# Rings of four buffers for split weights, and a later place in the code for the second memory split

## The chip, the cores and the metric

The kernel runs on one core of one Trainium2 chip. The metric is the device time of one execution in microseconds (us), the median of three runs. The engines are TensorE (PE, its weight loads PEld), VectorE (DVE), ScalarE (ACT), GpSimd (POOL) and SyncE (SP, which issues the weight loads from HBM here).

## The reference

A decoder trunk of two layers works on 512 tokens of width 1024, in float32. Each layer has a mixer, a cross-attention over 256 memory tokens and a SwiGLU feed-forward network (FFN) with 2816 hidden units, each behind an RMSNorm and with a residual add.

```python
def swiglu(h, w_gate_up, w_down):
    g, u = jnp.split(h @ w_gate_up, 2, axis=-1)
    return (jax.nn.silu(g) * u) @ w_down

for layer in range(DEPTH):                      # DEPTH = 2
    if layer % 2 == 0:                          # pooling mixer beside latent attention (MLA)
        x = x + even_mixer(rms_norm(x, ev_norm[j]), ...)
    else:                                       # Griffin: conv, gates, RG-LRU scan, GeLU gate
        x = x + odd_mixer(rms_norm(x, od_norm[j]), reset, ...)
    x = x + mem_cross_attention(rms_norm(x, xa_norm_x[layer]), mem, xa_norm_mem[layer], ...)
    x = x + swiglu(rms_norm(x, ffn_norm[layer]), ffn_w_gate_up[layer], ffn_w_down[layer])
return rms_norm(x, final_norm)
```

## The kernel before

Activations are kept transposed, features on the partitions: eight tiles of 128 x 512 for `x`. Each float32 operand is split into a high part `hi`, rounded to the type that TensorE takes in one pass, and the remainder `lo`. A product is then three matmuls per 128 rows of depth (`mm3`): L169 `hi` with `hi`, L170 `hi` of the weight with `lo` of the activation, L171 `lo` of the weight. ScalarE makes each `hi` by a copy (L101 for a weight, L156 for other tiles, L159 with a gain), VectorE makes each `lo` (L102, L157, L160).

`Weights.get` loads a block of weights into one of two raw buffers (`wraw`), on SP, and splits it into one buffer of the ring `whi` and one of the ring `wlo`. Both rings belong to the whole kernel: every projection of it and the fast FFN tiles draw from them. A buffer is free again when the last matmul that reads it has run.

The FFN has 22 hidden tiles per layer, in five parts of 4, 4, 4, 4 and 6. While a part's hidden tiles are made, the down projection of the part before it runs, two of its eight output tiles (names `s`) per hidden tile; its weights are the `dn` blocks (`dn_h`, `dn_l`), one block per two outputs. The last part has its down projection alone at the end of the FFN, one block per output. Tiles 5 to 21 of layer 0 and 5 to 15 of layer 1 are made by `fast`: two products of the full size are replaced by seven of a quarter of it, with 12 matmuls of 128 x 256 each. In the order of the code these are f1 (bank X, with names `mm`), f2 (Y, `tr`), f4 (Z, `att`), f5 (X), f7 (Z), f6 (X) and f3 (X). Their weights come in four splits (`parts`, names `sw_h` and `sw_l`): f1|f2 from a loaded half `gr`, f4|f6 from a sum `sa`, f5|f7 from a sum `sb`, and f3 from the other loaded half. With the `dn` block a fast tile takes five buffers of each ring. What I call a period is the work of one fast tile with its two down outputs.

The tile at the end of `fast` is multiplied with the SiLU of the gate and split (`hidden`; `act` in the trace), for the down projection.

Behind layer 0's last fast tile, `fastp.close()` gives up the pool of the fast tiles. `aside` is the function `ready` of the main program: it opens the pool `mg1`, loads the memory tokens into `keys` (four loads on SP) and splits them with the gain of layer 1's memory norm into `mg` (eight L159 on ScalarE, eight L160 on VectorE, of 128 x 256). `mg` is first read in the odd layer, by `mem_keys` (names `mg`, `xk_h`), whose products wait for banks that VectorE empties with `g` (L1044). L1057 multiplies gates and scanned states there, L1036 is the scan, and L278 the residual add anywhere.

No order of instructions is written out here. The scheduler of the tile framework takes the code's order as a list, estimates times, and gives each engine a fixed sequence; dependencies and free buffers decide which instruction is next in it.

Of the kernel before, what the change touches and what calls it, by code (L numbers as in the profile page):

```python
# [71 lines left out]
class Weights:  # L72


    def __init__(self, kern, ap, name, parts=None, low=None, into=None):
        self.kern, self.ap, self.name, self.into = kern, ap, name, into
        self.low = low or kern.nc.vector
        self.pools = parts or (kern.wraw, kern.whi, kern.wlo)
        self.n, _, self.F = ap.shape
        self.group = max(1, 1024 // self.F)  # L80
        self.raw = {}
        self.parts = {}
# [24 lines left out]
class Trunk:  # L107
    def __init__(self, ctx, tc, ins, out):
        self.ctx, self.tc, self.nc, self.ins, self.out = ctx, tc, tc.nc, ins, out
        pool = lambda name, bufs=1, **kw: ctx.enter_context(tc.tile_pool(name=name, bufs=bufs, **kw))  # L110
        self.cst = pool("cst")
        self.xp = pool("xp")
        self.kfp = pool("kfp")
        self.wraw = pool("wraw", 2)
        self.whi = pool("whi", 3)
        self.wlo = pool("wlo", 3)
        self.inp = pool("inp", 4)
        self.actp = pool("act", 16)
        self.tp = pool("tmp", 2)
        self.rp = pool("rp", 1)  # L120
        self.sm = pool("sm", 12)
        self.psum = pool("psum", 2, space=PSUM)
        self.uid = 0
        self.flip = 0
# [637 lines left out]
    def ffn(self, layer, nrm, nxt_spec, aside=None):  # L762
# [107 lines left out]
        def down(p, hs):  # L870
            nf = FFN_PARTS[p]
            W = Weights(self, ins[f"ffn_down{p}"], f"dn{layer}_{p}")
            n = D // (nf * P)
            return [lambda m=m: self.linear(W, layer * (KD // n) + m // n, hs, off=m % n * nf * P, bank="s")
                    for m in range(KD)]
# [4 lines left out]
        for p, nf in enumerate(FFN_PARTS):  # L880
            last = p == len(FFN_PARTS) - 1
            if last and final:
                fastp.close()
                pool = self.ctx.enter_context(self.tc.tile_pool(name="tail", bufs=1))
# [26 lines left out]
            for f in range(f0 + len(hs), f0 + nf):  # L911
                hs.append(fast(f, st) if f in FAST[not final] else plain(f))
                for _ in range(2):
                    if todo:
                        m = KD - len(todo)
# [5 lines left out]
            self.tail(Wd, hs, layer * KD, B)  # L921
            return None
        fastp.close()
        if aside:
            aside()
        nxt = self.next_norm(B, *nxt_spec)
        for m, run in enumerate(down(p, hs)):
            self.residual(m, run(), nxt)
        return nxt

    def odd(self, nrm, nxt_spec):
# [302 lines left out]
```

## Time and profile before

| | |
|---|---|
| median of three runs | 1410.14 us (1410.04 to 1410.41) |
| profiled execution | 1408.14 us |
| its span, first to last instruction | 1406.3 us |
| mean granted TensorE clock | 0.992 of full speed |
| TensorE busy | 1368.2 us, 97% of the span |
| VectorE busy | 910.8 us, 65% |
| ScalarE busy | 652.7 us, 46% |
| bytes moved by DMA | 139.40 MB, 99 GB/s on average |

Busy time of TensorE counts matmuls whose spans overlap, so 97% is not 97% of what it could do: the distance from one start to the next tells its pace. In the rows below, a time stands first for the start and then for the length; what is in brackets at the end is how long the engine was idle just before, and what ended that.

### The profile page before, as it was taken

The numbers are of one execution on the slowest core, as the hardware profiler recorded it, in microseconds if no ns is written. First come the engines' busy times: TensorE is split into PE (matmuls) and PEld (weight loads), VectorE is DVE, ScalarE is ACT, GpSimd is POOL, SyncE is SP. The second block draws the span as 40 slices with busy tenths as digits, with TensorE's granted clock in tenths as the row PEclk, the third lists the DMA queues.
The fourth block names the chain that finished last, engine by engine and source line by source line (L and its number), as shares of the span: only waits on it lengthen the run. The fifth ranks groups of instructions, "written<-read, shape, count | busy, mean of one in ns | idle before, by whom it ended". The sixth has DMA issues, their size and how long they took to land.

```text
span 1406.3 us, 19022 instructions
## 1 busy us (share of the span) xinstructions
PE 1368.2 (97%) x7496; PEld 1176.1 (84%) x7496; DVE 910.8 (65%) x1449; ACT 652.7 (46%) x1053; POOL 119.3 (8%) x131
## 2 busy tenths in 40 slices
PE   8899999999999999999999989999999999999998
PEld 7678788878888999989788878888888889998887
DVE  6787574545777767676868696445559676764343
ACT  6477653444444344444544754335445334443231
POOL 0431021003000000000110001211120000000001
PEclk9989999999999999999999999999999999999999
DMA  6231162323242332331232234322324233213231
GB/s 208 81 94 57 57 187 82 106 75 105 86 139 90 107 104 90 103 93 53 90 105 91 89 99 157 98 71 89 117 90 143 83 105 106 91 46 113 97 106 60
DMA packets 44970, 139.40 MB, mean 99 GB/s; under 512 B 5584, under 2 KB 9808, under 8 KB 44880
## 3 DMA queue, kind: packets, MB, share of 16 engines
q1 hardware_dynamic: 43440, 136.86, 30.2%
q10 hardware_dynamic: 1440, 1.32, 0.3%
q8 instruction: 59, 0.97, 0.3%
q14 instruction: 31, 0.25, 0.1%
HBM read 135.93 MB, written 2.10 MB: 98 GB/s over the span
## 4 chain that ended last, share of the span: by engine, by line
PE 81%; ACT 7%; DVE 5%; issue 3%; DMA 2%; POOL 0%; POOLq 0%; DVEq 0%; ACTq 0%
PE mm L169 14%; PE mm L170 13%; PE mm L171 13%; PE s L171 6%; PE att L169 6%; PE att L170 6%; PE att L171 5%; PE s L169 5%; PE s L170 5%; ACT sw_h L156 2%; ACT dn_h L101 1%; ACT t L855 1%; PE tr L170 1%; PE tr L169 1%; PE tr L171 1%
## 5 line engine op out<-in xcount | busy, mean ns | idle before, releaser
L169 PE MATMUL s<-act,dn_h 128*128 128x512 f32 x304 | 118.7, 391 | 2.1 <-ACT act L156 1.6
L170 PE MATMUL s<-act,dn_h 128*128 128x512 f32 x304 | 118.7, 390 | 0.6 <-DVE act L157 0.6
L171 PE MATMUL s<-act,dn_l 128*128 128x512 f32 x304 | 116.7, 398 | 0.0
L250 POOL TENSOR_TENSOR ssq<-ssq,t 128x512 f32<-128x512 f32 (+1 forms) x37 | 57.7, 1560 | 632.3 <-ACT t L249 632.0
L156 ACT CAST sw_h<-sa 128x1024 fp32r<-128x1024 f32 x28 | 29.4, 1049 | 138.3 <-PE s L170 131.5
L278 DVE TENSOR_TENSOR x<-s,x 128x512 f32<-128x512 f32 x72 | 49.5, 688 | 51.5 <-PE s L171 51.4
L101 ACT CAST gu_h<-gu_raw 128x1024 fp32r<-128x1024 f32 x32 | 33.6, 1051 | 85.6 <-PE mm L170 45.4
L171 PEld LDWEIGHTS s<-act,dn_l 128*128 128x128 f32 x304 | 57.0, 188 | 14.0 <-DVE dn_l L102 1.9
L169 PEld LDWEIGHTS s<-act,dn_h 128*128 128x128 f32 x304 | 57.2, 188 | 12.9 <-ACT act L156 2.1
L170 PEld LDWEIGHTS s<-act,dn_h 128*128 128x128 f32 x304 | 57.1, 188 | 12.1 <-DVE act L157 1.0
L101 ACT CAST dn_h<-dn_raw 128x1024 fp32r<-128x1024 f32 (+1 forms) x40 | 40.2, 1007 | 51.8 <-PE att L170 30.7
L171 PE MATMUL mm<-tb,sw_l 128*128 128x256 f32 x224 | 63.5, 284 | 0.0
L170 PE MATMUL mm<-tb,sw_h 128*128 128x256 f32 x224 | 63.4, 283 | 0.0
L169 PE MATMUL mm<-tb,sw_h 128*128 128x256 f32 x224 | 62.8, 281 | 0.0
L854 DVE TENSOR_TENSOR t<-att,pc 128x256 f32<-128x256 f32 x28 | 11.9, 424 | 77.2 <-PE att L171 77.2
L102 DVE TENSOR_TENSOR gu_l<-gu_raw,gu_h 128x1024 fp32r<-128x1024 f32 x32 | 39.2, 1224 | 25.4 <-ACT gu_h L101 24.9
L157 DVE TENSOR_TENSOR sw_l<-gr,sw_h 128x1024 fp32r<-128x1024 f32 (+1 forms) x56 | 53.2, 950 | 1.1 <-ACT sw_h L156 0.8
L156 ACT CAST sw_h<-gr 128x1024 fp32r<-128x1024 f32 (+1 forms) x56 | 46.4, 828 | 15.4 <-PE mm L170 6.1
L169 PE MATMUL mm<-act,gu_h 128*128 128x512 f32 x128 | 50.3, 395 | 0.0
L169 PE MATMUL mm<-act,xq_h 128*128 128x512 f32 x128 | 50.1, 391 | 0.0
L171 PE MATMUL mm<-act,xq_l 128*128 128x512 f32 x128 | 50.1, 391 | 0.0
L169 PE MATMUL att<-act,gu_h 128*128 128x512 f32 x128 | 50.0, 390 | 0.0
(478 smaller groups left out, 4462.1 us busy)
## 6 DMA issues: line engine op xcount, KB each, us to landing
gr<-in_ffn_gu_dram SPq DMA_DIRECT2D x56, 512.0 KB, 3.6
gu_raw<-in_ffn_gu_dram SPq DMA_DIRECT2D x32, 512.0 KB, 3.5
dn_raw<-in_ffn_down_dram SPq DMA_DIRECT2D x32, 512.0 KB, 3.5
xk_raw<-in_xa_w_k_dram SPq DMA_DIRECT2D x16, 512.0 KB, 3.5
xq_raw<-in_xa_w_q_dram SPq DMA_DIRECT2D x16, 512.0 KB, 3.5
xv_raw<-in_xa_w_v_dram SPq DMA_DIRECT2D x16, 512.0 KB, 3.5
xo_raw<-in_xa_w_o_dram SPq DMA_DIRECT2D x16, 512.0 KB, 3.6
odin_raw<-in_od_w_in_dram SPq DMA_DIRECT2D x16, 512.0 KB, 3.5
```

Of the source, the lines that this page charges most:

```text
L101: nc.scalar.copy(hi, src)
L102: self.low.tensor_sub(lo, src, hi[:, :].bitcast(F32))
L156: nc.scalar.copy(hi, src)
L157: nc.vector.tensor_sub(lo, src, hi.bitcast(F32))
L169: nc.tensor.matmul(out, wh, xh, start=begin and i == 0, stop=False, **kw)
L170: nc.tensor.matmul(out, wh, xl, start=False, stop=False, **kw)
L171: self.mm_ins = nc.tensor.matmul(out, wl, xh, start=False, stop=end and i == last, **kw).ins
L250: (low or nc.gpsimd).tensor_add(ssq[:, :n], ssq[:, :n], sq[:, :n])
L278: self.nc.vector.tensor_add(self.x[m], ps, self.x[m] if src is None else src)
L854: nc.vector.tensor_add(t[:, hi], Z, c[:, hi])
L855: nc.scalar.activation(t, t, AF.Silu)
```

## The change

Both rings of split weights get a fourth buffer. The call of `aside` moves from ahead of the last down projection of layer 0 to behind its second output tile.

```diff
@@ -112,8 +112,8 @@
         self.xp = pool("xp")
         self.kfp = pool("kfp")
         self.wraw = pool("wraw", 2)
-        self.whi = pool("whi", 3)
-        self.wlo = pool("wlo", 3)
+        self.whi = pool("whi", 4)
+        self.wlo = pool("wlo", 4)
         self.inp = pool("inp", 4)
         self.actp = pool("act", 16)
         self.tp = pool("tmp", 2)
@@ -921,11 +921,11 @@
             self.tail(Wd, hs, layer * KD, B)
             return None
         fastp.close()
-        if aside:
-            aside()
         nxt = self.next_norm(B, *nxt_spec)
         for m, run in enumerate(down(p, hs)):
             self.residual(m, run(), nxt)
+            if m == 1 and aside:
+                aside()
         return nxt
 
     def odd(self, nrm, nxt_spec):
```

The scheduler makes a new order from this. Three places of it matter below. In the rows, numbers tell buffers apart; what stands right of the arrow is read.

In the fast stage of layer 0 this stands on ScalarE, for one period; `pc` (L846, L850, L852) are copies of banks, `t0` (L855) is the SiLU, and 753, 755 and 776 are banks. Before:

```order
L846 COPY pc_756_4222<-mm_753_4219 128x256
L156 CAST act0_737_4155<-t1_736_4061 128x512
L156 CAST sw_h_751_4215<-gr_742_4195 128x512
L850 COPY pc_757_4223<-att_755_4221 128x256
L852 COPY pc_756_4222<-mm_753_4219 128x256
L101 CAST dn0_0_h2_4325<-dn0_0_raw2_4323 128x1024
L855 ACTIVATE t0_758_4224<-t0_758_4224 128x512
L156 CAST sw_h_766_4361<-gr_764_4357 128x1024
L156 CAST sw_h_769_4368<-sa_768_4365 128x1024
L156 CAST sw_h_772_4375<-sb_771_4372 128x1024
L846 COPY pc_779_4386<-mm_776_4383 128x256
```

After:

```order
L156 CAST sw_h_751_4215<-gr_742_4195 128x512
L156 CAST act0_737_4155<-t1_736_4061 128x512
L846 COPY pc_756_4222<-mm_753_4219 128x256
L101 CAST dn0_0_h2_4325<-dn0_0_raw2_4323 128x1024
L850 COPY pc_757_4223<-att_755_4221 128x256
L852 COPY pc_756_4222<-mm_753_4219 128x256
L156 CAST sw_h_766_4361<-gr_764_4357 128x1024
L855 ACTIVATE t0_758_4224<-t0_758_4224 128x512
L156 CAST sw_h_769_4368<-sa_768_4365 128x1024
L156 CAST sw_h_772_4375<-sb_771_4372 128x1024
L156 CAST sw_h_774_4379<-gr_765_4359 128x512
```

The down block's split `dn0_0_h2` moves ahead of the copies L850 and L852, and f1's split `sw_h_766` ahead of the SiLU. TensorE's order at the same place, from the end of f6 (`sw_h_746`) to the next tile's f1 (`sw_h_766`), before:

```order
L169 MATMUL mm_753_4219<-ta_694_3777,sw_h_746_4204 128x256
L170 MATMUL mm_753_4219<-ta_695_3778,sw_h_746_4204 128x256
L171 MATMUL mm_753_4219<-ta_694_3777,sw_l_747_4205 128x256
L169 MATMUL s_762_4329<-act0_668_3715,dn0_0_h2_4325 128x512
L170 MATMUL s_762_4329<-act0_669_3716,dn0_0_h2_4325 128x512
L169 MATMUL s_763_4343<-act0_668_3715,dn0_0_h2_4325 128x512
L170 MATMUL s_763_4343<-act0_669_3716,dn0_0_h2_4325 128x512
L169 MATMUL mm_776_4383<-act1_652_3676,sw_h_766_4361 128x256
L170 MATMUL mm_776_4383<-act1_653_3677,sw_h_766_4361 128x256
L169 MATMUL tr_777_4384<-act1_660_3696,sw_h_766_4361 128x256
```

After, from the end of f7 (`sw_h_749`) to the start of f6 (`sw_h_746`):

```order
L169 MATMUL att_755_4221<-act1_666_3711,sw_h_749_4211 128x256
L170 MATMUL att_755_4221<-act1_667_3712,sw_h_749_4211 128x256
L171 MATMUL att_755_4221<-act1_666_3711,sw_l_750_4212 128x256
L171 MATMUL s_762_4329<-act0_668_3715,dn0_0_l2_4326 128x512
L169 MATMUL s_762_4329<-act0_672_3725,dn0_0_h2_4325 128x512
L170 MATMUL s_762_4329<-act0_673_3726,dn0_0_h2_4325 128x512
L171 MATMUL s_762_4329<-act0_672_3725,dn0_0_l2_4326 128x512
L169 MATMUL s_762_4329<-act0_702_3851,dn0_0_h2_4325 128x512
L169 MATMUL mm_753_4219<-ta_676_3735,sw_h_746_4204 128x256
L170 MATMUL mm_753_4219<-ta_677_3736,sw_h_746_4204 128x256
```

The other ten matmuls of f6 and 13 of the down projection follow; then come its last two and the next tile's f1:

```order
L170 MATMUL s_763_4343<-act0_709_3922,dn0_0_h2_4325 128x512
L171 MATMUL s_763_4343<-act0_708_3921,dn0_0_l2_4326 128x512
L169 MATMUL mm_776_4383<-act1_652_3676,sw_h_766_4361 128x256
L170 MATMUL mm_776_4383<-act1_653_3677,sw_h_766_4361 128x256
L169 MATMUL tr_777_4384<-act1_660_3696,sw_h_766_4361 128x256
L170 MATMUL tr_777_4384<-act1_661_3697,sw_h_766_4361 128x256
L171 MATMUL mm_776_4383<-act1_652_3676,sw_l_767_4362 128x256
```

Before, f6 is followed by four matmuls of the down projection and then f1. After, f7 stands behind these four (not shown), f6 comes later and is split off by down matmuls on both sides, and the rest of the down projection stands ahead of f1.

The second place is the end of layer 0's FFN. On ScalarE before (`act0_1103` is the hidden tile of the last fast tile):

```order
L101 CAST dn0_4_h1_6809<-dn0_4_raw1_6807 128x768
L942 DMA t1_1139_7042<-in_positions_dram 128x512
L101 CAST dn0_4_h2_6842<-dn0_4_raw2_6840 128x768
L159 ACTIVATE mg_1106_6758<-keys_1105_6753,vecs_91 128x256 x8
L949 ACTIVATE sp_u_7046<-vecs_91 128x8
L156 CAST act0_1103_6745<-t1_1102_6651 128x512
L950 ACT_TABLE_LOAD
L950 ACTIVATE sp_u_7046<-sp_u_7046 128x8
L101 CAST dn0_4_h3_6875<-dn0_4_raw3_6873 128x768
```

After:

```order
L101 CAST dn0_4_h1_6784<-dn0_4_raw1_6782 128x768
L855 ACTIVATE t0_1101_6650<-t0_1101_6650 128x512
L101 CAST dn0_4_h2_6842<-dn0_4_raw2_6840 128x768
L942 DMA t1_1139_7042<-in_positions_dram 128x512
L101 CAST dn0_4_h3_6875<-dn0_4_raw3_6873 128x768
L159 ACTIVATE mg_1114_6823<-keys_1113_6818,vecs_91 128x256 x8
L949 ACTIVATE sp_u_7046<-vecs_91 128x8
L156 CAST act0_1103_6745<-t1_1102_6651 128x512
L950 ACT_TABLE_LOAD
L950 ACTIVATE sp_u_7046<-sp_u_7046 128x8
L101 CAST dn0_4_h4_6908<-dn0_4_raw4_6906 128x768
```

The eight `mg` splits stay in front of `sp_u` and the hidden tile's split; one more `dn` block, `dn0_4_h3`, comes ahead of them. TensorE before, the last rows ahead of the first matmul that reads the hidden tile (13 down matmuls stand from the end of f3 to there):

```order
L170 MATMUL s_1111_6813<-act0_1060_6452,dn0_4_h1_6809 128x512
L171 MATMUL s_1111_6813<-act0_1059_6451,dn0_4_l1_6810 128x512
L169 MATMUL s_1111_6813<-act0_1082_6615,dn0_4_h1_6809 128x512
L170 MATMUL s_1111_6813<-act0_1083_6616,dn0_4_h1_6809 128x512
L171 MATMUL s_1111_6813<-act0_1082_6615,dn0_4_l1_6810 128x512
L169 MATMUL s_1108_6782<-act0_1103_6745,dn0_4_h0_6778 128x512
L169 MATMUL s_1111_6813<-act0_1103_6745,dn0_4_h1_6809 128x512
```

After, from the end of f3 (`sw_h_1094`):

```order
L170 MATMUL mm_1096_6645<-tb_697_3782,sw_h_1094_6641 128x256
L171 MATMUL mm_1096_6645<-tb_696_3781,sw_l_1095_6642 128x256
L169 MATMUL s_1109_6788<-act0_1059_6451,dn0_4_h1_6784 128x512
L170 MATMUL s_1109_6788<-act0_1060_6452,dn0_4_h1_6784 128x512
L171 MATMUL s_1109_6788<-act0_1059_6451,dn0_4_l1_6785 128x512
L169 MATMUL s_1109_6788<-act0_1082_6615,dn0_4_h1_6784 128x512
L170 MATMUL s_1109_6788<-act0_1083_6616,dn0_4_h1_6784 128x512
L171 MATMUL s_1109_6788<-act0_1082_6615,dn0_4_l1_6785 128x512
L169 MATMUL s_1106_6757<-act0_1103_6745,dn0_4_h0_6753 128x512
L169 MATMUL s_1109_6788<-act0_1103_6745,dn0_4_h1_6784 128x512
```

Between f3 and the first reader of the hidden tile stand 6 down matmuls in place of 13; the other seven are ahead of f3.

The third place is in the odd layer on VectorE, where `g_1225` frees the bank for the first product of keys, and `g_1227` that for the second. Before:

```order
L1035 TENSOR_TENSOR i_1211_7631<-h7_7579,i_1211_7631 128x512
L1057 TENSOR_TENSOR h0_7134<-g_1213_7667,h0_7134 128x512
L1057 TENSOR_TENSOR h1_7177<-g_1215_7700,h1_7177 128x512
L1057 TENSOR_TENSOR h2_7220<-g_1217_7733,h2_7220 128x512
L1057 TENSOR_TENSOR h3_7263<-g_1219_7766,h3_7263 128x512
L1044 TENSOR_TENSOR g_1225_7865<-mm_1224_7840,R_1147_7098 128x512
L1057 TENSOR_TENSOR h4_7402<-g_1221_7799,h4_7402 128x512
L1036 SCALAR_TENSOR_TENSOR h6_7536<-r_1205_7601,i_1207_7610 128x512
L1057 TENSOR_TENSOR h5_7445<-g_1223_7832,h5_7445 128x512
L102 TENSOR_TENSOR xk1_l9_7935<-xk1_raw9_7932,xk1_h9_7934 128x1024
L1036 SCALAR_TENSOR_TENSOR h7_7579<-r_1209_7622,i_1211_7631 128x512
L1044 TENSOR_TENSOR g_1227_7898<-mm_1226_7873,R_1147_7098 128x512
```

After:

```order
L1044 TENSOR_TENSOR g_1225_7865<-mm_1224_7840,R_1147_7098 128x512
L102 TENSOR_TENSOR xk1_l10_7967<-xk1_raw10_7964,xk1_h10_7966 128x1024
L1036 SCALAR_TENSOR_TENSOR h5_7445<-r_1193_7488,i_1195_7497 128x512
L1035 TENSOR_TENSOR i_1211_7631<-h7_7579,i_1211_7631 128x512
L1036 SCALAR_TENSOR_TENSOR h6_7536<-r_1205_7601,i_1207_7610 128x512
L1057 TENSOR_TENSOR h0_7134<-g_1213_7667,h0_7134 128x512
L1057 TENSOR_TENSOR h1_7177<-g_1215_7700,h1_7177 128x512
L1057 TENSOR_TENSOR h2_7220<-g_1217_7733,h2_7220 128x512
L1057 TENSOR_TENSOR h3_7263<-g_1219_7766,h3_7263 128x512
L1057 TENSOR_TENSOR h4_7402<-g_1221_7799,h4_7402 128x512
L1057 TENSOR_TENSOR h5_7445<-g_1223_7832,h5_7445 128x512
L1036 SCALAR_TENSOR_TENSOR h7_7579<-r_1209_7622,i_1211_7631 128x512
```

The row that follows here is `g_1227`. `g_1225` moves ahead of an L1035 and four L1057; `g_1227` stays behind the same states, with the split `xk1_l10` added ahead of it.

## The prediction

> **What bounds the kernel now.** I began with the page's busy shares, then the clock by stretches, then the waits, and last the timeline of the places where the change moves instructions.
>
> ```profile
> span 1406.3 us, 19022 instructions
> ...
> PE 1368.2 (97%) x7496; PEld 1176.1 (84%) x7496; DVE 910.8 (65%) x1449; ACT 652.7 (46%) x1053; POOL 119.3 (8%) x131
> ```
>
> ```profile
> core 0: us, PE busy (x) PEld busy (x) DVE busy (x) ACT busy (x) POOL busy (x), PEclk, DMA share, GB/s
> 67.20:77.50 10.30, 7.56 (x21) 5.31 (x22) 8.34 (x20) 4.66 (x9) 5.71 (x5) 0.50 0.25 84
> ...
> 166.20:169.60 3.40, 3.40 (x12) 3.01 (x11) 1.41 (x3) 0.48 (x1) 0.00 (x0) 0.50 0.02 5
> 683.00:690.00 7.00, 4.41 (x17) 3.02 (x18) 6.63 (x18) 6.62 (x13) 0.32 (x1) 1.00 0.14 48
> ...
> 831.80:835.20 3.40, 3.24 (x15) 3.27 (x16) 3.40 (x7) 3.13 (x5) 0.00 (x0) 0.50 0.44 145
> ...
> 440.00:665.00 225.00, 222.82 (x1516) 203.84 (x1516) 160.76 (x239) 96.44 (x141) 0.00 (x0) 1.00 0.29 93
> ```
>
> TensorE carries the span, and the change takes no matmul away. It can gain or lose only where a matmul waits, or where the granted clock (the column after POOL) halves. Three stretches, of 10.3, 3.4 and 3.4 us, ran at 0.50. In the fast stage of layer 0 (440 to 665) VectorE works 160.76 of 225 us, so it is not the bound there.
>
> ```profile
> ACT sw_h L156 <- PE s L170: 138.1, 27, 5.4
> ...
> PEld mm L169 <- ACT sw_h L156: 14.9, 24, 1.4
> ...
> PEld mm L169 <- ACT sw_h L156: 7.8, 14, 0.6
> ```
>
> These rows are waits (us in total, times, longest). ScalarE's hi splits of fast tiles stand up to 5.4 us until a product has released a slot of the ring: that is the three buffers. TensorE's weight loads in turn wait 24 times for such a split, 14 of them from 440 to 665 us (the last row is of that window). Two of the 24 are the borders behind the first fast tile of each layer; 22 are regular, the 14 of layer 0 and 8 in layer 1. One of the regular ones, on ScalarE, VectorE and TensorE:
>
> ```profile
> 453.70 1.05 ACT L101 CAST dn_h<-dn_raw 128x1024 fp32r<-128x1024 f32 x1 [0.94 <-PE att L170]
> ...
> 455.19 1.03 ACT L156 CAST sw_h<-gr 128x1024 fp32r<-128x1024 f32 x1
> ...
> 455.62 1.22 DVE L102 TENSOR_TENSOR dn_l<-dn_raw,dn_h 128x1024 fp32r<-128x1024 f32 x1
> ...
> 455.06 0.39 PE L169 MATMUL s<-act,dn_h 128*128 128x512 f32 x1
> ...
> 455.52 0.39 PE L169 MATMUL s<-act,dn_h 128*128 128x512 f32 x1
> 455.75 0.39 PE L170 MATMUL s<-act,dn_h 128*128 128x512 f32 x1
> 456.27 0.39 PE L169 MATMUL mm<-act,sw_h 128*128 128x256 f32 x1
> 456.49 0.28 PE L170 MATMUL mm<-act,sw_h 128*128 128x256 f32 x1
> ...
> 456.73 0.28 PE L170 MATMUL tr<-act,sw_h 128*128 128x256 f32 x1
> 456.89 0.50 PE L171 MATMUL s<-act,dn_l 128*128 128x512 f32 x1
> 457.23 0.40 PE L169 MATMUL s<-act,dn_h 128*128 128x512 f32 x1
> ```
>
> Read the starts, since matmuls overlap. A 128x512 follows in 0.23 us, a 128x256 in 0.12 (two steps in the 0.24 from 456.49 to 456.73). From 455.75 to 456.49 are 0.74 us where one of each (0.35) would do: 0.39 lost to f1's hi split. It can begin only when the product f6 lets go of its slot, about 455.1, and from there until f1 stand four down matmuls: 4 x 0.23 = 0.92 us of cover for a split of 1.03. From 456.73 to 457.23 are 0.50 where 0.35 would do: 0.15 lost to the down block's lo split (455.62 plus 1.22 is 456.84).
>
> **The change, part by part.** No instruction is added or taken away. The rings get longer, and the scheduler orders the work anew.
>
> *Fast stages.* In the order of after, f1's split waits for f7, and between f7's end and f1 TensorE has 20 down matmuls and f6's 12: 20 x 0.23 + 12 x 0.12 = 6.0 us of cover for 1.03. The down block's hi split waits for f2's release, in front of f4 and f5: 24 x 0.12 = 2.9 us until its first use, against 1.05 and two small copies queued near it. Its lo split is wanted four down matmuls and f7 later, at 2.9 + 0.9 + 1.4 = 5.2 us, against 1.05 + 1.22. f4|f6's split waits for f6, and 15 down matmuls and 36 short ones stand before its use (7.8 us); f5|f7's waits for the last down matmul, with 48 short ones before its use (5.8 us). Each needs about 2.3 us for hi and lo. On SP the loads of gate-up halves now stand behind a down block's; there DMA works 0.29 of the time, so I price that at nothing; without that cover f1 would wait for its load. The gain of a period lies between 0.29 (0.52 from 455.75 to 456.27, less 0.23) and 0.54 (0.39 + 0.15). I take 0.45, nearer the upper end, as both waits lose their cause and a little may come back at other borders. 22 periods make -9.9 us (-6.4 to -11.9).
>
> *The first borders and the last.* The border behind the first fast tile loses more:
>
> ```profile
> 423.95 0.39 PE L169 MATMUL mm<-act,sw_h 128*128 128x256 f32 x1 [0.94 <-ACT sw_h L156]
> ```
>
> Its split stood behind a SiLU that waited, by way of VectorE, for a load. After places the tile later, but the load is not earlier. Of 2 x 0.94 I take about half, with a little for the last fast tile: -1.3 us (0 to -2.3).
>
> *The moved call.* The loads of memory and the eight mg splits are what it issues. The loads stand early on SP in both orders. The mg tile lies in the space of the closed fast pool, so its splits wait for f3, the last fast product, wherever the call stands. In both orders they are ahead of the hidden tile's hi split on ScalarE:
>
> ```profile
> 679.85 0.84 ACT L101 CAST dn_h<-dn_raw 128x768 fp32r<-128x768 f32 x1 [4.71 <-PE mm L170]
> 680.59 3.30 ACT L159 ACTIVATE mg<-keys,vecs 128x256 fp32r<-128x256 f32 x8
> ...
> 683.90 0.60 ACT L156 CAST act<-t 128x512 fp32r<-128x512 f32 x1
> ...
> 685.10 0.68 DVE L157 TENSOR_TENSOR act<-t,act 128x512 fp32r<-128x512 f32 x1
> ...
> 679.77 0.39 PE L171 MATMUL s<-act,dn_l 128*128 128x512 f32 x1
> ...
> 682.53 0.39 PE L171 MATMUL s<-act,dn_l 128*128 128x512 f32 x1
> 684.55 0.73 PE L169 MATMUL s<-act,dn_h 128*128 128x512 f32 x2 [1.63 <-ACT act L156]
> 685.83 0.50 PE L170 MATMUL s<-act,dn_h 128*128 128x512 f32 x1 [0.55 <-DVE act L157]
> ```
>
> From 679.77 TensorE has 13 down matmuls until 682.76, then idles 1.63 us for the hidden hi split and 0.55 for its lo. In after the chain on ScalarE is the same length (a down split, mg, hidden), but only 6 down matmuls are left behind f3, as seven more go ahead of it. 7 x 0.23 = 1.6 us of cover are gone: +1.6 us (0 if the scheduler's order is made good by an earlier f3; 2.0 with knock-on waits). The gap becomes about 3.2 us, then 0.55. Here the clock comes in. Idle times of 1.81 and 2.09 within seven us (rows of the odd layer, below) and of 2.54 and 1.39 (MLA, below) were each followed by a half-rate stretch, while 1.63 + 0.55 here were not (1.00 from 683 to 690). 3.2 + 0.55 is like those with one. A 3.4 us stretch at half rate does 1.7 us of work less: +1.7 (0 to 5.1, by the 10.3 us stretch).
>
> The Trainium skill ("TensorE: Matmul & The Clock Gate", section "Why this matters for your kernels") sets the bound at idle gaps of more than about 3 us. By that rule two shorter gaps would cost no clock; the trace shows 0.50 behind gaps of 1.81 and 2.09, and none as long as 3. With the new gap at 3.2 us the rule leaves it at the edge, and without the drop the sum would be 1.7 us lower.
>
> *Odd layer.* Between Griffin and the second cross-attention TensorE waits for banks that VectorE frees with g L1044:
>
> ```profile
> 826.75 0.36 PE L169 MATMUL mm<-mg,xk_h 128*128 128x256 f32 x1 [1.81 <-issue]
> ...
> 829.59 0.28 PE L171 MATMUL mm<-mg,xk_l 128*128 128x256 f32 x1
> 831.96 0.55 PE L169 MATMUL mm<-mg,xk_h 128*128 128x256 f32 x1 [2.09 <-DVE g L1044]
> ...
> 822.98 0.67 DVE L1035 TENSOR_TENSOR i<-h,i 128x512 f32<-128x512 f32 x1
> 823.56 2.49 DVE L1057 TENSOR_TENSOR h<-g,h 128x512 f32<-128x512 f32 x4
> 825.97 0.68 DVE L1044 TENSOR_TENSOR g<-mm,R 128x512 f32<-128x512 f32 x1
> ...
> 831.15 0.66 DVE L1044 TENSOR_TENSOR g<-mm,R 128x512 f32<-128x512 f32 x1
> ```
>
> In after the first of these g stands ahead of four L1057 and one L1035, 3.2 us earlier, so the 1.81 us gap goes. The second stands behind one more lo split of a key block (priced as the 1.22 us row of dn_l), so its bank comes about 1.1 us later, and what was two gaps is one of about 5 us. What counts is the second: +1.1 us. Lower bound -2, if VectorE's earlier work catches up; upper +4.5, if the half-rate stretch grows from 3.4 to 10.3 us on top. I take +1.0.
>
> *MLA.* The order changes from row to row, with fillers in other gaps, behind
>
> ```profile
> 67.80 0.90 PE L573 MATMUL s<-act,act 128*128 128x128 f32 x2 [2.54 <-ACT act L156]
> ...
> 70.09 0.79 PE L169 MATMUL att<-evv_h,ckh 128*128 128x512 f32 x1 [1.39 <-DVE t L537]
> ```
>
> A value product now stands in the first gap, but ScalarE's queue, which sets it, is as long. -0.3 us (-4 if the 10.3 us stretch becomes a short one, +4 if the idle times near 160 grow).
>
> *Sum:* -9.9 - 1.3 + 1.6 + 1.7 + 1.0 - 0.3 = -7.2 us. The profiled execution took 1408.14 us, 1.8 more than its span and 2.0 less than the median of the runs, 1410.14; I take the sum from the median: 1402.9, say 1403.0. A change within 0.2% (2.8 us) is about what the measurement can't tell from none.
>
> **The rivals.**
> - *The half rate takes it back.* The stretches at the last down projection and in the odd layer last 10.3 us rather than 3.4, each 3.4 us dearer: 1403.0 + 6.8 = 1409.8, no change. For it: one such stretch stands behind idle times of 2.54 and 1.39. Against: behind 1.81 and 2.09 it was 3.4.
> - *Slower: the wait moves to the down block.* In after ScalarE's hi split of the down block follows the hidden split and a copy, which wait for VectorE. If it comes more than 2.9 - 1.05 = 1.85 us behind f2's release, TensorE stops at the down matmul instead. Beyond this point each 0.1 us costs 22 x 0.1 = 2.2. With 0.45 us of it nothing of the gain remains; with 0.5 it is 1403.0 + 22 x 0.5 = 1414.0. Against: VectorE's 160.76 of 225 us.
> - *More gain.* The gap behind f3 draws no half rate, and MLA's 10.3 us stretch shrinks to 3.4: 1403.0 - 1.7 - 3.4 = 1397.9. For it: the value product in the first gap.
> - *Half of it.* The regular waits halve (-5.0 rather than -9.9), and the odd layer's second gap loses another us: about 1409, no change. For it: splits in strict queues, where one late operation holds all behind it.
>
> The second part of the change as such does nothing by all of these: the mg splits stay where they were.
>
> **How the numbers follow.** My forecast has 0.52 (its own range 1400 to 1407), the half rate 0.14, slower 0.12, more gain 0.12, half of it 0.10. Faster: 0.52 + 0.12 + 0.02 = 0.66. Same: most of the half rate and of the half gain, 0.21. Slower: 0.12 and a bit of the half rate, 0.13. The range of 1398 to 1411 leaves out the slower rival and a little at the lower end.
>
> **What would show it.** Right: the waits of TensorE's loads for sw_h vanish from the fast stages, the period falls from about 16.1 to 15.6 us, and no wait for dn_h takes their place. The idle time in front of the hidden tile's down matmul grows from 1.63 to about 3.2 us, with mg x8 in front of the hidden split; the clock behind it reads 0.50. In the odd layer one gap of about 5 us replaces two. Wrong: a regular wait for dn_h or dn_l in the fast stages, loads of gr that land late behind a down block's on SP, or half-rate stretches in MLA longer than 10.3 us.

## The result and the profile after

The changed kernel took 1396.73 us, the median of four runs (1395.43 to 1400.26); the kernel before, beside it, 1410.09. The ratio is 0.9914, with a 95% interval of 0.9898 to 0.9930. The forecast was 1403.0 us, in a range of 1398 to 1411. The direction was right; the gain, 13.4 us between medians, was nearly twice the 7.1 that I gave, and the time lies 1.3 us below the range. Run again later, beside other kernels on one chip, it took 1397.57 against 1409.29, a gain of 11.7. Between the two profiled executions the span fell by 11.5 us, from 1406.3 to 1394.8; this is what can be followed in rows.

The page's first rows after, and the stretches that answer to those shown of before (columns as there; the clock stands after POOL):

```profile
span 1394.8 us, 19076 instructions
...
PE 1359.9 (97%) x7496; PEld 1178.4 (84%) x7496; DVE 927.0 (66%) x1449; ACT 655.1 (47%) x1053; POOL 122.0 (9%) x131
```

```profile
68.20:75.00 6.80, 5.03 (x13) 3.77 (x14) 5.13 (x7) 2.61 (x5) 6.72 (x6) 0.50 0.42 125
440.00:665.00 225.00, 225.00 (x1583) 211.36 (x1583) 172.46 (x244) 102.45 (x149) 0.00 (x0) 1.00 0.28 91
...
675.80:682.60 6.80, 6.35 (x14) 4.61 (x15) 6.37 (x16) 4.66 (x8) 1.37 (x1) 0.50 0.31 73
822.60:829.40 6.80, 3.50 (x16) 3.54 (x17) 6.80 (x11) 4.00 (x7) 0.00 (x0) 0.50 0.13 34
```

In the fast stage TensorE is now busy for all of the 225 us, and does 1583 matmuls there in place of 1516. The share of busy time, 97%, did not move at all: the 11.5 us are invisible in it. The waits in the same window (total, times, longest):

```profile
ACT sw_h L156 <- PE s L170: 32.8, 14, 2.3
ACT sw_h L156 <- PE mm L170: 31.4, 28, 1.3
ACT sw_h L156 <- PE att L170: 26.3, 14, 1.9
```

ScalarE still stands for slots, 90 us in all where it was 82; but none of TensorE's loads waits for sw_h any more. A wait of an engine that is early is harmless. From f1 to f1, TensorE in the timeline:

```profile
440.52 0.28 PE L169 MATMUL mm<-act,sw_h 128*128 128x256 f32 x1
...
455.88 0.39 PE L171 MATMUL s<-act,dn_l 128*128 128x512 f32 x1
456.10 0.28 PE L169 MATMUL mm<-act,sw_h 128*128 128x256 f32 x1
```

The period is 15.58 us here (15.59 on the average of the 22), and f1 follows the down matmul in front of it at 0.22 us, without a wait. Before it was 16.06 on the average (15.91 to 16.21); one began with the next row, and its end is the row of 456.27 in the prediction:

```profile
440.14 0.38 PE L169 MATMUL mm<-act,sw_h 128*128 128x256 f32 x1
```

Behind the last fast tile, on ScalarE, VectorE and TensorE:

```profile
670.25 0.84 ACT L101 CAST dn_h<-dn_raw 128x768 fp32r<-128x768 f32 x1 [5.32 <-PE mm L170]
670.99 3.30 ACT L159 ACTIVATE mg<-keys,vecs 128x256 fp32r<-128x256 f32 x8
...
674.29 0.60 ACT L156 CAST act<-t 128x512 fp32r<-128x512 f32 x1
...
674.95 0.74 PE L169 MATMUL s<-act,dn_h 128*128 128x512 f32 x2 [3.23 <-ACT act L156]
676.24 0.79 PE L170 MATMUL s<-act,dn_h 128*128 128x512 f32 x1 [0.56 <-DVE act L157]
676.83 0.63 PE L171 MATMUL s<-act,dn_l 128*128 128x512 f32 x1
```

The gap is 3.23 us, then 0.56, as forecast, and at half rate a matmul of 0.39 us shows as 0.63. In the odd layer one gap stands in the place of two:

```profile
825.89 0.55 PE L169 MATMUL mm<-mg,xk_h 128*128 128x256 f32 x1 [6.23 <-DVE g L1044]
...
820.36 3.68 DVE L1057 TENSOR_TENSOR h<-g,h 128x512 f32<-128x512 f32 x6
823.95 1.22 DVE L1036 TENSOR_TENSOR_SCAN h<-r,i 128x512 f32<-128x512 f32 x1
825.08 0.67 DVE L1044 TENSOR_TENSOR g<-mm,R 128x512 f32<-128x512 f32 x1
```

To see where the 11.5 us went, I cut both traces at matmuls that have the same work ahead of them:

| part | before, us | after, us | difference | forecast |
|---|---|---|---|---|
| start to the first query matmul of cross-attention 0 (set-up, MLA) | 212.03 | 211.17 | -0.9 | -0.3 |
| cross-attention 0, to the first FFN matmul | 139.66 | 137.99 | -1.7 | 0 |
| layer 0, last plain weight to the wait behind the last fast tile | 275.5 | 266.8 | -8.7 | |
| layer 1, last plain weight to the tail | 269.9 | 264.4 | -5.5 | |
| the two together: all fast stages | | | -14.2 | -11.2 |
| the wait behind the last fast tile, to the last gate matmul of the odd layer | 141.4 | 144.2 | +2.8 | +3.3 |
| from there to the odd layer's output projection | 30.0 | 32.8 | +2.8 | +1.0 |
| the rest | | | -0.4 | 0 |

The first row is not safe to read: in the nine traces whose order is the changed kernel's up to there (this one and those of `ring4_only`, `changed_again`, `mg_behind`, `mg_late`, `mg_late_again`, `gate_first`, `comb` and `xk_pool` below) this part took from 211.2 to 216.2 us. Much of what differs between runs of one kernel arises there.

### The profile page after: what moved, and what is told of

It reads as the page before. It is cut to its first block, busy times and chain, and to the rows that moved or that the text cites. A ratio compares the mean times of both kernels' runs of the same rounds, so it can differ in the third digit from the quotient of the medians.

```text
span 1394.8 us, 19076 instructions
## 1 busy us (share of the span) xinstructions
PE 1359.9 (97%) x7496; PEld 1178.4 (84%) x7496; DVE 927.0 (66%) x1449; ACT 655.1 (47%) x1053; POOL 122.0 (9%) x131
## 4 chain that ended last, share of the span: by engine, by line
PE 87%; DVE 5%; ACT 3%; issue 2%; DMA 0%; POOL 0%; POOLq 0%; DVEq 0%; ACTq 0%
PE mm L169 14%; PE mm L170 14%; PE mm L171 14%; PE s L171 6%; PE s L170 6%; PE s L169 6%; PE att L169 6%; PE att L170 6%; PE att L171 6%; PE tr L170 1%; PE tr L171 1%; PE tr L169 1%; DVE xk_l L102 1%; DVE act L157 1%; PE att L680 1%
## 5 line engine op out<-in xcount | busy, mean ns | idle before, releaser
L170 PEld LDWEIGHTS s<-act,dn_h 128*128 128x128 f32 x304 | 57.9, 190 | 11.7 <-DVE act L157 1.0
L171 PEld LDWEIGHTS s<-act,dn_l 128*128 128x128 f32 x304 | 57.9, 190 | 10.4
L156 ACT CAST sw_h<-sb 128x1024 fp32r<-128x1024 f32 x28 | 29.4, 1048 | 65.8 <-PE s L170 58.2
L102 DVE TENSOR_TENSOR dn_l<-dn_raw,dn_h 128x1024 fp32r<-128x1024 f32 (+1 forms) x40 | 46.8, 1171 | 14.5 <-ACT dn_h L101 14.1
L278 DVE TENSOR_TENSOR x<-mm,x 128x512 f32<-128x512 f32 x24 | 16.4, 691 | 51.7 <-PE mm L171 51.7
```

The source lines that it names most:

```text
L102: self.low.tensor_sub(lo, src, hi[:, :].bitcast(F32))
L156: nc.scalar.copy(hi, src)
L170: nc.tensor.matmul(out, wh, xl, start=False, stop=False, **kw)
L171: self.mm_ins = nc.tensor.matmul(out, wl, xh, start=False, stop=end and i == last, **kw).ins
L278: self.nc.vector.tensor_add(self.x[m], ps, self.x[m] if src is None else src)
```

## The experiments

**The rings without the moved call.** The edit is the first half of the change: `whi` and `wlo` at four, `aside` where it was. In the two traces every engine's order of work is the same, apart from buffer numbers.

> Both rings at four, the call of aside left where it was before. Theory (the rings alone make the time, the moved call does nothing, since every engine's order is that of the changed kernel): 1396 to 1399 us, the regular waits of TensorE's loads for sw_h gone, and the same 3.2 us gap behind the last fast tile. Rival (the later call is part of the gain, or of the 3.2 us gap): a gap of 1.6 us as before, and a time more than 2 us away from the changed kernel's 1396.7.

Measured: 1398.16 us (1396.92 to 1399.14), ratio 0.9926 (0.9909 to 0.9942), an interval that overlaps the changed kernel's; the gap behind the last fast tile was 3.22 us. So the rings make the time, and the moved call changes neither an order nor a time that can be told.

**One ring at a time.** The first, `hi4`:

```diff
-        self.wlo = pool("wlo", 4)
+        self.wlo = pool("wlo", 3)
```

> whi at four, wlo at three. Theory (the hi splits' slots are what the fast stages wait for): f1's wait is gone from every period, and 1397 to 1401 us; a rest of at most 0.15 us a period may stay with the down block's lo split, since the lo ring is short. Rival (lo slots hold it as much): the regular waits stay or move to a lo split, and the time is within 3 us of 1410.

Measured: 1422.55 us (1421.79 to 1427.89), ratio 1.0105 (1.0084 to 1.0126): slower than before. Neither theory had that time; the rival had it right that the wait would move to a lo split. The waits from 440 to 665 us of this kernel:

```profile
DVE sa L828 <- DMA gr<-in_ffn_gu_dram: 42.9, 13, 3.8
...
PEld s L171 <- DVE dn_l L102: 14.0, 13, 1.6
PE s L171 <- DVE dn_l L102: 12.1, 14, 1.4
```

f1's hi split is no longer waited for, but VectorE stands 3.2 us in each period for a load of gr, and the down block's lo split, four places behind it in VectorE's queue, comes late for TensorE; a period takes about 16.6 us. One period on VectorE:

```profile
465.19 0.69 DVE L157 TENSOR_TENSOR sw_l<-gr,sw_h 128x512 fp32r<-128x512 f32 x1 [0.18 <-PE tr L171]
...
469.38 0.69 DVE L828 TENSOR_TENSOR sa<-gr 128x512 f32<-128x512 f32 x1 [3.16 <-DMA gr<-in_ffn_gu_dram]
...
471.52 1.21 DVE L102 TENSOR_TENSOR dn_l<-dn_raw,dn_h 128x1024 fp32r<-128x1024 f32 x1
```

f3's lo split waits for a slot of the short lo ring (until f2 is done). As it reads gr, the buffer of gr comes free only at 465.9, and the load, 3.7 us from issue to landing, arrives at about 469.4. This is the slower rival of the prediction, a wait for the down block in every period, by another way: not a late hi split but a late load.

The second, `lo4`, is the other half, with `whi` at three and `wlo` at four.

> whi at three, wlo at four, the call of aside moved. Theory (the hi ring binds; the order of every engine is nearly that of before): 1409 to 1411 us, with the 0.13 us gaps at every period's f1 as before. Rival (the lo ring or the moved call brings part of the gain): below 1406 us.

Measured: 1409.22 us (1406.28 to 1411.95), ratio 1.0004 (0.9994 to 1.0015), with the regular waits as before (13 of TensorE's loads for sw_h, 7.3 us). The lo ring alone, with the moved call, brings nothing.

**The chain by way of the load.** If that reading of `hi4` holds, one more buffer for gr must mend it, with the lo ring left at three (the tag is shared with the line that holds the normed input of the FFN, whose count goes to five as well; not shown):

```diff
-                r = st.tile([P, D], F32, name=self.nm("gr"), tag="sraw", bufs=4)
+                r = st.tile([P, D], F32, name=self.nm("gr"), tag="sraw", bufs=5)
```

> whi at four, wlo at three, and five buffers instead of four for the loaded gate-up halves gr. With whi four and wlo three the kernel took 1422.6 us: VectorE stood 3.2 us per period for a load of gr, and the down block's lo split behind it came 0.8 us late for TensorE. Theory (the short lo ring delays f3's lo split, which holds a buffer of gr, so that the next load is issued late): with one buffer more the load is early again, the waits for gr and dn_l go, and 1397 to 1404 us. Rival (the lo slots are waited for themselves, whatever the loads do): dn_l or sw_l is still waited for in each period, 1415 us or more.

Measured: 1398.42 us (1396.78 to 1399.35), ratio 0.9923 (0.9907 to 0.9939). The waits for gr and for dn_l are gone from the list of the window. So the hi ring's fourth buffer is what the fast stages lacked; the lo ring's is needed only because a lo split that waits holds a load buffer. Against `hi4` the scheduler moved a small part of the rows, most of them in the fast stages; on VectorE the sums of gr (L828, L829) are among these. Against the changed kernel both have another order in most stages. So this is the chain's likely reading, not a proof that nothing else differs.

**The mg splits behind the last fast tile.** `mg_behind` holds them back until the hidden tile's hi split has been issued on ScalarE:

```diff
-            nc.scalar.copy(hi, src)
+            self.hi_ins = nc.scalar.copy(hi, src).ins
...
+        hid = self.hi_ins
...
             if m == 1 and aside:
-                aside()
+                with tc.issue_after(hid):
+                    aside()
```

> The changed kernel, with the eight mg splits put behind the hidden tile's hi split on ScalarE. Theory (the 3.2 us gap behind the last fast tile is ScalarE's queue, mg x8 of 3.30 us ahead of the hidden split, and the 6.8 us at half clock follow from that gap): the gap falls to about 1 us, no half-rate stretch behind it, and 5 to 7 us less than the changed kernel, about 1390 to 1392. Rival 1 (the half rate comes from elsewhere): the gap goes, the stretch stays, 3 us less. Rival 2 (the hidden tile itself is late, by VectorE): the gap stays at 2.5 us or more and the time is the changed kernel's.

Measured: 1394.05 us (1393.83 to 1395.43), ratio 0.9896 (0.9882 to 0.9911). The 3.23 us gap went altogether, but a new wait stands four matmuls behind the first row here:

```profile
673.50 0.50 PE L170 MATMUL s<-act,dn_h 128*128 128x512 f32 x1 [0.58 <-DVE act L157]
...
676.08 0.65 PE L169 MATMUL s<-act,dn_h 128*128 128x512 f32 x1 [1.38 <-DVE x L278]
```

The mg lo splits on VectorE now stood ahead of the residual add that empties a bank, and a half-rate stretch of 3.4 us remained. By the medians the gain is 2.7 us, and 4.1 against `ring4_only`, which ran beside it with the changed kernel's order; I had expected 5 to 7, since I had looked at one queue of the two.

`mg_late` puts them behind the split of the fifth output tile instead (`m == 4`, and that tile's hi split in place of `hid`).

> The changed kernel, with the mg splits behind the hi split of the fifth output tile of the last down projection (hi on ScalarE; the lo halves on VectorE follow it). Putting them only behind the hidden split left a wait of 1.38 us for a residual add that stood behind five mg lo splits on VectorE, and a half-rate stretch of 3.4 us. Theory (the mg splits in both queues are the whole loss behind the last fast tile): idle time there below 1 us in all, clock 1.00 from 665 to 700 us, 5 to 7 us less than the changed kernel's 1396.7, about 1390 to 1392. Rival (the mg splits only move their wait to the last outputs or the odd layer's first products): 1394 to 1397 us, with a new gap near 690 us.

Measured: 1393.47 us (1391.72 to 1394.90), ratio 0.9883 (0.9866 to 0.9899), 3.3 us below the changed kernel by the medians and not the 5 to 7 expected. Run again beside the changed kernel on one chip:

> The changed kernel once more, beside the next one on one chip. 1395 to 1398 us, with the half-rate stretches at the same places (MLA, behind the last fast tile, odd layer) but of other lengths, 3.4 or 6.8 us, as they were for the same order with the call left in its place.

> The changed kernel with the mg splits behind the fifth output's split, once more. If the 5.5 us that its trace lost behind the last fast tile are its worth, it is 4 to 6 us below the changed kernel on this chip; if the median of before (1393.5 against 1396.7) tells it, about 3.

1397.57 (1395.73 to 1398.33) and 1392.59 us (1390.71 to 1395.92): 5.0 us less. The intervals of the two ratios, 0.9900 to 0.9929 and 0.9868 to 0.9901, just meet. The traces tell it better without the set-up and MLA: from the first query matmul of cross-attention 0 to TensorE's last matmul the changed order took 1176.2, 1174.9 and 1174.7 us (changed kernel, once more, `ring4_only`), `mg_late` 1170.7 and 1170.6. Of this second trace, the place behind the last fast tile and the clock of 20 us around it:

```profile
671.75 0.73 PE L169 MATMUL s<-act,dn_h 128*128 128x512 f32 x2
673.06 0.50 PE L170 MATMUL s<-act,dn_h 128*128 128x512 f32 x1 [0.58 <-DVE act L157]
...
674.72 0.50 PE L169 MATMUL s<-act,dn_h 128*128 128x512 f32 x1 [0.46 <-DVE x L278]
...
670.00:690.00 20.00, 18.92 (x82) 14.75 (x81) 18.61 (x43) 13.26 (x20) 4.18 (x3) 1.00 0.34 111
```

1.04 us of idle time is left of 3.79, and no half-rate stretch. This version takes less time than both kernels, 16.7 us less than the one before. So the moved call could have gained something, had it held the mg splits back; its place in the code alone did not.

**The odd layer.** `gate_first` puts the eight L1057 on VectorE behind the last g, so that the 3.68 us ahead of g in the row above are gone (`self.g_ins` is the last L1044).

```diff
+                with tc.issue_after(self.g_ins):
+                    nc.vector.tensor_mul(hs[m], t, hs[m])
-                nc.vector.tensor_mul(hs[m], t, hs[m])
```

> The changed kernel, with the eight products L1057 on VectorE put behind the last g (L1044), which frees the bank for the second product of keys. Theory (the 6.2 us gap in the odd layer is VectorE's order, six L1057 of 3.68 us ahead of g): the gap falls to about 2.5 us, the half-rate stretch there shrinks to 3.4 us or goes, and 3 to 6 us less than the changed kernel, 1391 to 1394. Rival (VectorE is full in this stretch, so that what is put behind is waited for later): the gap falls, but as much comes back as waits for keys or for the hidden tiles h, within 1.5 us of 1396.7.

Measured: 1399.16 us (1394.84 to 1400.86), ratio 0.9923 (0.9903 to 0.9942), 2.4 us above the changed kernel, with intervals that overlap; neither theory's range has it. The gap fell by 3.6 us to 2.62, the half-rate stretch there to 3.4 us, and 3.17 us came back one product later as a wait for keys L378. Together with mg_late, as `comb`:

> mg_late and gate_first together. Theory (two separate places, both on the path that sets the end): the gains add, 8 to 13 us less than the changed kernel, 1384 to 1389. Rival (one of the two is given back by the other or was none): the better of the two alone.

Measured: 1393.65 us (1391.80 to 1394.91), ratio 0.9887 (0.9873 to 0.9902): that of mg_late alone. The rival's mechanism was right: VectorE is full here (42.43 of 45 us from 800 to 845 in the changed kernel), and its order only chooses which product waits.

`xk_pool` takes the key blocks' lo splits from VectorE and gives them to GpSimd, by the argument that names the engine:

```diff
-            self.mem_keys(1, self.mg, 0, KD, None)
+            self.mem_keys(1, self.mg, 0, KD, nc.gpsimd)
```

> The changed kernel, with the lo splits of the eight key blocks of the odd layer on GpSimd instead of VectorE; TensorE's order is the same. Theory (VectorE is full there): three splits of 1.13 us fewer ahead of g, so that the 6.2 us gap falls by about 3 us, and 2 to 5 us less than 1396.7. Rival (GpSimd is too slow: a product of keys takes 2.9 us, and a split there more than that): new waits for xk_l of more than 1 us each, and a time at or above 1396.7.

Measured: 1404.55 us (1401.18 to 1405.93), ratio 0.9960 (0.9946 to 0.9974): the rival's sign, but not for its reason. No new wait was for xk_l; VectorE itself got slower. GpSimd and VectorE in this kernel:

```profile
803.61 2.81 POOL L102 TENSOR_TENSOR xk_l<-xk_raw,xk_h 128x1024 fp32r<-128x1024 f32 x1 [50.76 <-DVE h L1036]
810.89 3.99 POOL L102 TENSOR_TENSOR xk_l<-xk_raw,xk_h 128x1024 fp32r<-128x1024 f32 x1 [4.47 <-ACT xk_h L101]
...
804.07 0.69 DVE L1044 TENSOR_TENSOR g<-mm,R 128x512 f32<-128x512 f32 x1
804.67 2.30 DVE L1035 TENSOR_TENSOR i<-h,i 128x512 f32<-128x512 f32 x1
...
812.66 2.76 DVE L1031 SCALAR_TENSOR_TENSOR h<-t,h 128x512 f32<-128x512 f32 x1
815.35 0.68 DVE L1044 TENSOR_TENSOR g<-mm,R 128x512 f32<-128x512 f32 x1
```

An L1035 of 0.68 us took 2.30 and an L1031 of 0.67 took 2.76 while a split ran on GpSimd; both ended about 0.55 us after that split. (Two operations at the start of each split took their usual time. The second split took 3.99 us where the shortest of the eight took 2.40, as if it had waited for them; but spans on GpSimd are rough.) What VectorE was spared, it lost again by standing still. TensorE waited 4.89 us for a tile of ScalarE's (h, L985) that stood behind the L1031 of 2.76, and 6.93 for g where it had been 6.23, and the half-rate stretches here were 3.4 and 10.2 us in place of one of 6.8.

## Why the prediction was right or wrong

- *Fast stages, the regular waits: right.* 0.45 us per period was forecast, to 15.6 us; 22 periods from 16.06 to 15.59 are 0.47 each, 10.4 us against 9.9. The order of after and the durations of before were enough to see that no split would come late.
- *The first borders and the last tile: the step that failed.* I gave 1.3 us, 2.3 at most. The fast stages are 14.2 us shorter in all, so 3.8 fall outside the regular periods. I had taken half of two gaps of 0.94 (the second, in layer 1, is 0.84) and little for the last tile, with the argument that the load was not earlier. In fact these gaps went, and so did one of 0.37 at the last tile (the changed trace has no gap over 0.1 us from the first fast tile to the last), with the lost pace around them. Cut at places where the same matmuls lie ahead in both traces, the two borders are shorter by 1.4 and 1.3 us and the two ends by 0.9 and 0.4. The load did not have to be earlier: in the order of after the SiLU that waits for it stands behind f1's split, which ran 1.4 us earlier against the first FFN matmul (at 69.8 us in place of 71.2), and 20 more matmuls stand in front of that f1, so that it comes 3.5 us later (75.8 in place of 72.3). Here the start-to-start distances should have been added up, as I did for the period, and not the gaps alone. The two gaps of before that the prediction does not show:

```profile
664.54 0.39 PE L171 MATMUL mm<-act,sw_l 128*128 128x256 f32 x1 [0.37 <-DVE sw_l L157]
...
1108.32 0.38 PE L169 MATMUL mm<-act,sw_h 128*128 128x256 f32 x1 [0.84 <-ACT sw_h L156]
```

- *Cross-attention 0: 0 forecast, -1.7 found.* It was not in the sum. The kernel `lo4`, with nearly the order of before, needed 138.3 us for this part, before 139.7, the changed kernel 138.0. So 1.4 of it are not the change. They are one load of an output-projection block, which took 4.93 us from issue to landing before, where the median of such loads is 3.6: ScalarE's split waited longer for it there (first row) than in `lo4` (second row), and TensorE's delay begins there.

```profile
301.92 1.05 ACT L101 CAST xo_h<-xo_raw 128x1024 fp32r<-128x1024 f32 x1 [3.56 <-DMA xo_raw<-in_xa_w_o_dram]
...
299.80 1.05 ACT L101 CAST xo_h<-xo_raw 128x1024 fp32r<-128x1024 f32 x1 [2.19 <-DMA xo_raw<-in_xa_w_o_dram]
```

- *The measure: -2.0.* I worked on an execution 2.0 us faster than the median of the kernel before, and took the sum off the median. The changed kernel's profiled execution (1396.59) was at its median. So 2 us of the miss are the reference, not a term.
- *The moved call: right.* The mg splits stayed, the gap grew to 3.23 (forecast 3.2) and 0.56 (0.55), with a half-rate stretch behind it. In this trace it lasted 6.8 us, and 3.4 in two others of the same order, as I had it. At its end the changed kernel had lost 4.0 us to the one before, and 2.5 and 2.7 in those two, where I had 3.3; in this trace 1.2 came back in the odd layer, up to its last gate matmul, which leaves the +2.8 of the table.
- *Odd layer: right in kind, too small.* One gap took the place of two, 6.23 us where I had about 5. The two were 3.90 together, so the gap alone is +2.3 us in place of +1.1: the first g, which I had 3.2 us earlier, saved TensorE only the 1.81 of the first gap, and from it to the second g VectorE, never idle, needed 9.3 us in place of 5.2. A wait for keys right behind grew from 0.32 to 0.81. The longer stretch at half rate, 6.8 us in place of 3.4, cost only 0.1: it begins at 822.6, inside the gap, and TensorE works from 825.9. (Before, it began at 831.8, also inside the gap.) The whole came to +2.8 instead of +1.0, inside the bounds that I gave.
- *MLA: -0.9, forecast -0.3,* with one stretch of 6.8 us at half rate in the place of 10.3 and 3.4; by the spread under the table no reading rests on it. Of the two idle times that I put ahead of the 10.3 us, the second ended at 70.09, inside the stretch that began at 67.2.
- *The rivals.* "More gain" came nearest to the time (1397.9) by the wrong way: of its two steps, no half rate behind f3 did not happen, and MLA's stretch shrank by half of what it said. "The half rate takes it back" had the two stretches at 10.3 us; they lasted 6.8, and the one in the odd layer lay half in a gap. "Half of it" needed half of the regular waits to stay; none did. "Slower" did not happen here; `hi4` ran into a wait of its kind, by the late loads of gr that I had named as a sign of being wrong.

The miss thus has three parts of known size: 3.0 us of the fast stages, 2.3 of cross-attention and MLA, of which 1.4 are the late load and 0.6 are within the spread of runs, and 2.0 of the reference (0.4 are spread elsewhere); 1.3 us worse than forecast in the odd layer and behind the last tile stand against them. These two happen to make the miss smaller than its parts. What stays open is why that load came later in one run than in the other.

## What to carry to other kernels

When a ring holds work back, count what stands between the release of a slot and the first use of what is made in it, in matmuls; the cover here was 0.92 us for a 1.03 us split, and by the order that one buffer more allows it is 6.0. Where one operation fills two rings, follow the shorter one to what it holds: the lo ring alone gained nothing, the hi ring alone lost 1% through a load buffer that was freed late. And a call's place in the code need not be its place in an engine's queue: here moving it changed no order at all, and the mg splits gained 4 to 5 us only when tied behind an instruction of their own engine.

## What the runs showed of the hardware

The half-rate stretches were 3.4, 6.8 or 10.2 us, multiples of 3.41, in all traces, but for the one that the end of the kernel cuts off. The same order with the same 3.2 us gap drew 6.8 us in one execution and 3.4 in two others; the row above is of the first, this one of the kernel with the rings alone:

```profile
677.90:681.10 3.20, 3.06 (x6) 2.00 (x7) 2.76 (x12) 2.51 (x6) 0.00 (x0) 0.50 0.00 0
681.30:685.00 3.70, 3.70 (x18) 3.06 (x17) 3.70 (x6) 1.84 (x4) 1.39 (x1) 1.00 0.70 178
```

So a gap costs its length and, by luck, some more: 1.3 to 1.5 us lie between these executions at this place, and 0.1 us was all that a stretch of 6.8 us instead of 3.4 cost in the odd layer, where it began inside the gap. The Trainium skill ("TensorE: Matmul & The Clock Gate", section "Part 1: The HAM clock gate") states a window of 3413 ns that runs free of the kernel; the traces agree in the lengths, and in that one order drew different ones. The rule of the Trainium skill to leave no idle gap above about 3 us between bursts of matmuls ("TensorE: Matmul & The Clock Gate", section "Why this matters for your kernels") is not enough here: gaps of 1.81 and 2.09 drew a stretch in the kernel before.

I had not expected GpSimd to stop VectorE for 2 us at a time. The Trainium skill ("Trainium Architecture — The Big Picture", section "What this means for kernel authors") calls the pair of ports that the two share an exclusive lock; the rows of 0.68 us operations that took 2.30 and 2.76, to about 0.55 us behind the split's end, agree. No run here tells which operations the lock holds back: two at the start of each split kept their length.
